# Other start addresses for the SBUF tiles, and two buffers for the local bias tiles

## The chip, the cores and the metric

The kernel runs on one core of one Trainium2 chip. The metric is device time in microseconds (us) for one execution. TensorE (PE; its weight loads are PEld), VectorE (DVE), ScalarE (ACT) and GpSimd (POOL) compute; SyncE (SP) does no arithmetic here and issues most of the DMAs, in program order. SBUF has 128 partitions; every address below is a byte offset within a partition.

## What is computed

Two transformer blocks one after the other on 512 tokens of width 1024, in float32, batch 1:

```
x = first_block(x):   h = rms_norm(x); z = h @ w_in
                      o_fox: 8 heads, causal softmax attention with a forget gate
                      o_nsa: 8 heads; compressed, selected and window attention, summed with gates
                      x += (sigmoid-gated sum of o_fox @ w_br_fox and o_nsa @ w_br_nsa) @ w_out
                      x += relu(rms_norm(x) @ w_ff1)**2 @ w_ff2 ; rms_norm
y = second_block(x):  16 meta tokens ahead of x (528 positions)
                      o_a: 8 heads, sliding window of 128 with sinks and a relative bias
                      o_b: 8 heads on latent keys, each query on its top 256 positions by an index score
                      h += (gate_a * (o_a @ w_branch_a) + gate_b * (o_b @ w_branch_b)) @ w_out
                      h += (silu(rms_norm(h) @ w_gate) * (rms_norm(h) @ w_up)) @ w_down ; rms_norm
```

## The kernel before

Activations lie transposed: eight tiles of 128 features by 512 tokens. To reach float32 accuracy each dense product is three matmuls (`mm3`, line 655): every operand is split into a high part (ScalarE's cast, names in `h`) and a low part (the difference, names in `l`).

All weights stand in HBM as one list of panels (`wall`, 128 partitions x 1024 floats) in the order of use. For each panel there are three steps: `w_load_to` (line 567) issues the DMA into one of three `wr` tiles on SyncE; `w_split_to` (line 604) has ScalarE cast it to `wh` and VectorE or GpSimd subtract to get `wl`, three of each; `dense` (line 660) multiplies, `wh` and `wl` being the stationary operand and an activation tile the moving one of up to 512 columns. Panels are loaded three ahead and split two ahead. A planner in the kernel (`chain`, `pick`, `tick`) keeps a list of small steps with estimated due times and writes them out between the matmuls; it decides the order in which the instructions of every engine stand in the program. It knows nothing of addresses.

SBUF is laid out by pools, in the order in which `build` opens them (lines 2540 to 2546): constants from 16512 to 22784 (`pvt`, `cst` with 640 floats, `ones`, `G` and rings of small tiles), then `rkeep` with two slots of 2112 bytes for the norm factors (`Ra`, `Rb`, `R1`, `Rt`, `Rc`, `Rd`; `Rt` has 528 floats), then the weight pool from 27008 (three each of `wr`, `wh`, `wl`, 4096 bytes), the `tmp` ring from 63872 (four of 2048), and the `u` pool from 72064: 34 slots of 2112 bytes, since the tiles with the meta tokens have 528 floats. The pools of the stages follow from 143872, one set per stage: attention of block 1, FFN 1, attention of block 2, FFN 2. Their `v` slots have 2048 bytes. So, modulo 512: `wr`, `wh`, `wl` and `tmp` start at 384; `rkeep` slots at 256 and 320; `v` slots at 0; `u` slots, 2112 = 4 x 512 + 64 apart, at all multiples of 64.

In block 1's attention and in both gate stages the activations that are multiplied (`xh`, `xl`) are `u` tiles, as `mgh`, `mgl`, `oh`, `ol` are; in both FFNs all of them (`xh`, `xl`, `hh`, `hl`) are `v` tiles. The last eight panels of the second FFN (`2fd*_2`) are split into `u` tiles, named `wk`, and multiplied on halves of 256 columns.

Sliding-window attention of block 2 (`unA_S`, line 2092) runs head by head. Each head needs a bias tile `wa` of 128 x 256, read from DRAM scratch by a DMA on SyncE (`wa_load`, line 2300). Heads 0 and 1 are loaded ahead; head h + 2's load is written at the start of head h:

```python
                if h + 2 < 8:
                    self.wa_load(h + 2)
            nm, l, Pt = u["m"], u["l"], u["P"]
            ...
            wa = self.wa[h]
```

The four VectorE instructions of a head that read it (`P<-pss,wa,nsink`, in `softmax_piece`) come later in the program. `wa` tiles form a ring of three; a load into a slot waits until the slot's last reader is done. Weight loads `wr` stand between the `wa` loads in SyncE's order.

Of the kernel before, what the change touches and what calls it, by code (L numbers as in the profile page):

```python
# [8 lines left out]
F32 = mybir.dt.float32  # L9
# [8 lines left out]
P = 128  # L18
T = 512
# [2 lines left out]
DH = 64  # L22
NMETA = 16
TK = T + NMETA
HT = TK // 2
NEG = -1e30
EPS = 1e-6
# [226 lines left out]
class Prog:  # L254
# [34 lines left out]
    def kk(self, dt=F32):  # L289
        return self.kpool.tile([P, TK], dt, name=self.nm("kk"), tag="kk", bufs=self.nk)  # L290

# [386 lines left out]
    def dense_meta(self, name, evac, M=P, tag="d"):  # L678
# [3 lines left out]
        for k in range(KD):  # L682
# [3 lines left out]
            for n, (w, x) in enumerate(((a, xh), (a, xl), (b, xh))):  # L686
                for e in range(2):
                    self.mms(ps[e][0:M, 0:HT], w, x[:, HT * e:HT * e + HT], k == 0 and n == 0, k == KD - 1 and n == 2)
            yield
        evac(ps)  # L690

    def scaled_meta(self, dst, ps, rows=P, M=NMETA):

        nc = self.nc
        R, w = self.Rf, HT - M
        nc.vector.tensor_mul(dst[0:rows, 0:w], ps[0][0:rows, M:HT], R[0:rows, M:HT])
        nc.vector.tensor_mul(dst[0:rows, w:w + HT], ps[1][0:rows, 0:HT], R[0:rows, HT:TK])
        if M:
# [978 lines left out]
    def x_steps(self, X, m, src, g, sts, pool, meta=False):  # L1677

        if meta:
            hi, lo = self.XM[m] = pool(F32R, (P, TK), name="xh"), pool(F32R, (P, TK), name="xl")  # L1680

# [3 lines left out]
            self.chain(("xm", m), c, after=("mt",), prio=3)  # L1685
            hi, lo = hi[:, NMETA:TK], lo[:, NMETA:TK]
        else:
# [47 lines left out]
    def block1(self):  # L1735
        nc, tc = self.nc, self.tc
        self.XD, self.X, self.merged = {}, self.Xk, {}
        self.xl = tuple(("X", k) for k in range(8))
        self.block1_attention()
        with ExitStack() as c:  # L1740
            self.vpool = c.enter_context(tc.tile_pool(name="vf1", bufs=1))
            self.pk = self.pk2
            self.nv = self.nvf
            x = []
            for k in range(8):
                t = self.u(name="xr")
                nc.scalar.dma_start(t, self.I["xT"][P * k:P * k + P])
                x.append(t)
            self.XD = {}
            self.R = self.rkeep.tile([P, T], F32, name="Rb", tag="R", bufs=2)  # L1750
            self.R2 = self.v(name="R2")
            self.norm("R", 0, self.xl, lambda: self.R[:])
            self.w_out("wo", x, lambda m: self.x_steps(self.XD, m, x[m], self.pv("g_mlp", m), [(0, None)], self.v))
            X2, self.XM = {}, {}
            gg = self.small([P, 8])
            nc.vector.tensor_mul(gg, self.pv("g_final", 0, 8), self.pv("g2", 0, 8))
            x2 = tuple(("x", k) for k in range(8))
            N = {}
            st = {}

            def norms():

                N["R1"] = self.rkeep.tile([P, T], F32, name="R1", tag="R", bufs=2)
                self.Rf = self.rkeep.tile([P, TK], F32, name="Rt", tag="R", bufs=2)
                N["R"] = self.Rf[:, NMETA:TK]
                self.meta_prep(self.Rf)
                self.norm("R1", 0, x2, lambda: N["R1"][:])
                self.norm("pb", 1, x2, None, evac=lambda ps: nc.scalar.copy(N["R"], ps))
                self.chain("Rt", s2, *self.rstd_steps(lambda: st["t"][:], T, D, out=lambda: N["R"][:]), s3,
                           after=("pb", "R1"))  # L1770

            def s2():
                t = st["t"] = self.tmp()
                nc.vector.tensor_mul(t, N["R1"], N["R1"])
                nc.vector.tensor_mul(t, t, N["R"])

            def s3():
                nc.vector.tensor_mul(N["R"], N["R"], N["R1"])

            def after(m):  # L1780
                def store():
                    nc.sync.dma_start(self.xscr[m], x[m])
                return self.x_steps(X2, m, x[m], gg[:, m:m + 1], [(0, None), (1, self.pv("g_final", m))],
                                    self.u, True) + [store]
            self.ffn1(x, after, norms)
            self.ensure(*x2)
            self.R = N["R"]
            self.chain("R", lambda: None, after=("Rt",))
            self.chain("resid", lambda: nc.sync.dma_start(self.rscr, N["R1"]), after=("R1",))
            self.X = lambda k: (self.ensure(("x", k), ("xm", k)), X2[k])[1]  # L1790
# [507 lines left out]
        u["done"](ps)  # L2298

    def wa_load(self, h):  # L2300
        t = self.mpool.tile([P, 256], F32, name=self.nm("wa"), tag="wa", bufs=3)
        self.nc.sync.dma_start(t, self.diagonals(self.v2scr, h, W_UB, 256))
        self.wa[h] = t

# [233 lines left out]
    def build(self):  # L2538
        nc, tc, ctx = self.nc, self.tc, self.ctx
        self.cpool = ctx.enter_context(tc.tile_pool(name="const", bufs=1))  # L2540
        self.rkeep = ctx.enter_context(tc.tile_pool(name="rkeep", bufs=1))
        self.wpool = ctx.enter_context(tc.tile_pool(name="w", bufs=1))
        self.tpool = ctx.enter_context(tc.tile_pool(name="t", bufs=1))
        self.upool = ctx.enter_context(tc.tile_pool(name="u", bufs=1))
        self.dpool = ctx.enter_context(tc.tile_pool(name="dram", bufs=1, space=DRAM))
        self.pp = ctx.enter_context(tc.tile_pool(name="ps", bufs=1, space=PSUM))
        ctx.enter_context(tc.manual_schedule())
        self.pvt = self.cpool.tile([P, NPV], F32, name="pvt")
        nc.sync.dma_start(self.pvt, self.I["vecs"])
        cst = self.cpool.tile([P, T + P], F32, name="cst")  # L2550
        self.cst, self.mw, self.ident = cst, cst[:, 0:T], cst[:, T:T + P]
        self.ones = self.cpool.tile([P, P], F32, name="ones")
        nc.vector.memset(self.ones, 1.0)
        self.one = self.ones[:, 0:1]
        self.tc.nc.scalar.preload_act_table_set("natural_log_exp_and_others")
        self.G = self.cpool.tile([P, 4, 24], F32, name="G")
        self.cscr = self.dpool.tile([8, 6, T], F32R, name="cscr")
        self.xscr = self.dpool.tile([8, P, T], F32, name="xscr")
        self.rscr = self.dpool.tile([P, T], F32, name="rscr")
        self.vascr = self.dpool.tile([8, W_ASC], F32, name="vascr")  # L2560
        self.v1scr = self.dpool.tile([8, 640], F32, name="v1scr")
        self.v2scr = self.dpool.tile([16, W_UB + W_UA], F32, name="v2scr")
        t = self.tmp(F32R)
        nc.vector.memset(t[0:16].bitcast(F32), 1.0)
        nc.gpsimd.dma_start(self.cscr[:, 2], t[0:8])
        nc.gpsimd.dma_start(self.cscr[:, 3], t[8:16])
        self.w_init()
        self.block1()
        self.block2()
# [38 lines left out]
```

## Time and profile before

| | |
|---|---|
| median of 3 runs | 1590.37 us (1586.13 to 1592.13) |
| the profiled execution | 1588.41 us |
| its span, first to last instruction | 1586.6 us |
| busy TensorE, VectorE, ScalarE, GpSimd | 97%, 57%, 49%, 16% |
| mean granted TensorE clock | 0.991 |
| DMA | 149.34 MB, mean 94 GB/s |

A line of the profile names an engine, an operation and its tiles as out<-in, with buffer numbers left out. Line 242 stands at all of them, since a helper records every operation, so the tiles tell them apart. For a matmul the names after the arrow are the moving operand and the stationary one (the weights), in this order.

### The profile page before, as it was taken

The numbers are of one execution on the slowest core, as the hardware profiler recorded it, in microseconds if no ns is written. First come the engines' busy times: TensorE is split into PE (matmuls) and PEld (weight loads), VectorE is DVE, ScalarE is ACT, GpSimd is POOL, SyncE is SP. The second block draws the span as 40 slices with busy tenths as digits, with TensorE's granted clock in tenths as the row PEclk, the third lists the DMA queues.
The fourth block names the chain that finished last, engine by engine and source line by source line (L and its number), as shares of the span: only waits on it lengthen the run. The fifth ranks groups of instructions, "written<-read, shape, count | busy, mean of one in ns | idle before, by whom it ended". The sixth has DMA issues, their size and how long they took to land.

```text
span 1586.6 us, 19934 instructions
## 1 busy us (share of the span) xinstructions
PE 1540.4 (97%) x7400; PEld 1254.5 (79%) x7400; DVE 909.5 (57%) x1781; ACT 775.1 (49%) x1475; POOL 253.3 (16%) x184
## 2 busy tenths in 40 slices
PE   7999999999999999999998899999899999999997
PEld 3788888878878888888877788778687888888887
DVE  5686677762654243455467998576566332336445
ACT  5676687975343232322444784677434222232233
POOL 3343211111210000000044124411131000000001
PEclk9999999999999999999999999999999999999999
DMA  4444321113423333222243222320142223323311
GB/s 154 131 143 137 109 67 61 59 48 101 151 81 99 99 94 93 94 93 93 95 140 79 69 79 82 116 85 14 40 153 94 93 93 99 99 91 109 124 50 54
DMA packets 50545, 149.34 MB, mean 94 GB/s; under 512 B 6652, under 2 KB 10364, under 8 KB 50448
## 3 DMA queue, kind: packets, MB, share of 16 engines
q1 hardware_dynamic: 44496, 138.89, 27.4%
q0 software_dynamic: 3360, 4.46, 1.4%
q10 hardware_dynamic: 2592, 4.72, 0.9%
q8 instruction: 58, 0.95, 0.2%
q14 instruction: 39, 0.32, 0.1%
HBM read 138.37 MB, written 4.67 MB: 90 GB/s over the span
## 4 chain that ended last, share of the span: by engine, by line
PE 88%; DVE 7%; ACT 2%; DMA 2%; issue 1%; SPq 0%; ACTq 0%; POOL 0%; DVEq 0%; POOLq 0%
PE psd L242 74%; PE pss L242 5%; PE pso L242 4%; PE pst L242 4%; DVE sct L242 1%; DVE tmp L242 1%; DVE x L242 1%; DVE sq L242 1%; DMA x<-xT 1%; DVE sm L242 1%; ACT tmp L242 1%; DVE P L242 1%; DVE xl L242 1%; DVE pt L242 0%; ACT xh L242 0%
## 5 line engine op out<-in xcount | busy, mean ns | idle before, releaser
L242 PE MATMUL psd<-xh,wh 128*128 128x512 f32 (+2 forms) x1128 | 452.0, 401 | 8.3 <-ACT xh L242 8.3
L242 PE MATMUL psd<-xh,wl 128*128 128x512 f32 (+2 forms) x1128 | 443.6, 393 | 1.6 <-DVE wl L242 1.6
L242 PE MATMUL psd<-xl,wh 128*128 128x512 f32 (+2 forms) x1128 | 443.9, 394 | 0.4 <-DVE xl L242 0.3
L242 ACT CAST wh<-wr 128x1024 fp32r<-128x1024 f32 (+1 forms) x232 | 241.7, 1043 | 343.6 <-PE psd L242 211.1
L242 POOL TENSOR_TENSOR wl<-wr,wh 128x1024 fp32r<-128x1024 f32 x72 | 178.4, 2478 | 514.3 <-ACT wh L242 467.3
L242 PEld LDWEIGHTS psd<-xh,wh 128*128 128x128 f32 (+1 forms) x1128 | 212.5, 188 | 56.9 <-ACT xh L242 9.8
L242 DVE TENSOR_TENSOR wl<-wr,wh 128x1024 fp32r<-128x1024 f32 (+1 forms) x160 | 196.0, 1225 | 101.2 <-ACT wh L242 99.1
L242 PEld LDWEIGHTS psd<-xh,wl 128*128 128x128 f32 (+1 forms) x1128 | 212.4, 188 | 51.1 <-DVE wl L242 2.0
L242 PEld LDWEIGHTS psd<-xl,wh 128*128 128x128 f32 (+1 forms) x1128 | 212.6, 188 | 47.7 <-issue 2.4
L242 ACT ACTIVATE P<-P,sm 128x256 f32<-128x256 f32 (+7 forms) x319 | 165.8, 545 | 27.0 <-DVE sm L242 26.5
L242 PE MATMUL psd<-hh,wh 128*128 128x512 f32 x384 | 151.6, 395 | 0.0
L242 PE MATMUL psd<-hl,wh 128*128 128x512 f32 x384 | 151.5, 395 | 0.0
L242 PE MATMUL psd<-hh,wl 128*128 128x512 f32 x384 | 151.5, 395 | 0.0
L242 POOL TENSOR_TENSOR sq<-sq,tmp 128x512 f32<-128x512 f32 (+1 forms) x32 | 39.8, 1243 | 429.5 <-ACT tmp L242 426.8
L242 PEld LDWEIGHTS psd<-hh,wh 128*128 128x128 f32 x384 | 72.4, 188 | 17.0
L242 PEld LDWEIGHTS psd<-hh,wl 128*128 128x128 f32 x384 | 72.3, 188 | 16.9
L242 PEld LDWEIGHTS psd<-hl,wh 128*128 128x128 f32 x384 | 72.3, 188 | 16.8
L242 DVE TENSOR_TENSOR pt<-pst,pt 128x384 fp32r<-128x384 f32 (+3 forms) x144 | 69.3, 498 | 16.5 <-ACT pt L242 15.5
L242 ACT ACTIVATE tmp<-psd 128x512 f32<-128x512 f32 x32 | 19.1, 598 | 111.1 <-PE psd L242 111.0
L242 DVE TENSOR_TENSOR tmp<-tmp 128x512 f32<-128x512 f32 (+1 forms) x33 | 22.7, 686 | 87.7 <-ACT tmp L242 87.7
L242 ACT CAST pt<-pst 128x384 fp32r<-128x384 f32 (+3 forms) x144 | 58.5, 439 | 15.8 <-PE pst L242 14.5
L242 PE MATMUL pst<-cst,P 128*128 128x128 f32 (+1 forms) x416 | 62.3, 277 | 2.6 <-DVE pt L242 2.6
(368 smaller groups left out, 2286.2 us busy)
## 6 DMA issues: line engine op xcount, KB each, us to landing
wr<-wall SPq DMA_DIRECT2D x231, 512.0 KB, 3.5
wr<-wall SPq DMA_DIRECT2D x8, 384.0 KB, 3.0
kk<-v2scr SPq DMA_DIRECT2D x8, 264.0 KB, 4.4
x<-xT SPq DMA_DIRECT2D x8, 256.0 KB, 8.4
wb<-v1scr SPq DMA_DIRECT2D x8, 256.0 KB, 3.6
xr<-xT ACTq DMA_DIRECT2D x8, 256.0 KB, 4.5
xscr<-xr SPq DMA_DIRECT2D x8, 256.0 KB, 2.1
x<-xscr ACTq DMA_DIRECT2D x8, 256.0 KB, 4.0
```

The source lines that it names most:

```text
L242: return f(*a, **k)
```

## The change

The row of constants gets 64 floats (256 bytes) of which nothing is used, the norm-factor pool is opened after the `u` pool, `Rt` grows from 528 to 560 floats, and `wa` gets two buffers.

```diff
+CPAD = 64
...
-                self.Rf = self.rkeep.tile([P, TK], F32, name="Rt", tag="R", bufs=2)
+                self.Rf = self.rkeep.tile([P, TK + 32], F32, name="Rt", tag="R", bufs=2)
...
-        t = self.mpool.tile([P, 256], F32, name=self.nm("wa"), tag="wa", bufs=3)
+        t = self.mpool.tile([P, 256], F32, name=self.nm("wa"), tag="wa", bufs=2)
...
         self.cpool = ctx.enter_context(tc.tile_pool(name="const", bufs=1))
-        self.rkeep = ctx.enter_context(tc.tile_pool(name="rkeep", bufs=1))
         self.wpool = ctx.enter_context(tc.tile_pool(name="w", bufs=1))
         self.tpool = ctx.enter_context(tc.tile_pool(name="t", bufs=1))
         self.upool = ctx.enter_context(tc.tile_pool(name="u", bufs=1))
+        self.rkeep = ctx.enter_context(tc.tile_pool(name="rkeep", bufs=1))
...
-        cst = self.cpool.tile([P, T + P], F32, name="cst")
+        cst = self.cpool.tile([P, T + P + CPAD], F32, name="cst")[:, 0:T + P]
```

By these sizes the constants end at 22784 + 256 = 23040 = 45 x 512, and the weight pool starts there; `tmp` starts at 59904 = 117 x 512, the `u` pool at 68096 = 133 x 512, its slots still 2112 apart. The norm factors take 2 x 2240 bytes from 139904 (128 past a multiple of 512; the second slot 320 past one), and the pools of the stages start at 144384 = 282 x 512, 512 bytes above their old start 143872 = 281 x 512. The ring of `wa` gives back 1024 bytes at the end of block 2's pools.

## Rows read from the trace of the kernel before

**Rows 1.** The page: busy time by engine, and shares of the chain that ended last.
```profile
PE 1540.4 (97%) x7400; PEld 1254.5 (79%) x7400; DVE 909.5 (57%) x1781; ACT 775.1 (49%) x1475; POOL 253.3 (16%) x184
...
PE 88%; DVE 7%; ACT 2%; DMA 2%; issue 1%; SPq 0%; ACTq 0%; POOL 0%; DVEq 0%; POOLq 0%
```

**Rows 2.** The chain in order of time: start us, us, what, count.
```profile
347.93 111.72 PE psd L242 x483
...
464.15 314.41 PE psd L242 x1353
...
949.55 14.06 PE psd L242 x61
...
1541.97 16.09 PE psd L242 x134
```

**Rows 3.** Groups by line, TensorE, each form: count, busy us, mean ns, idle before.
```profile
L242 PE MATMUL psd<-xh,wh 128*128 128x512 f32 x1096 | 440.8, 402 | 0.0
...
L242 PE MATMUL psd<-hh,wh 128*128 128x512 f32 x384 | 151.6, 395 | 0.0
...
L242 PE MATMUL psd<-mgh,wh 128*128 128x512 f32 x128 | 50.6, 395 | 0.0
```

**Rows 4.** Groups by line, TensorE's weight loads, each form.
```profile
L242 PEld LDWEIGHTS psd<-hh,wh 128*128 128x128 f32 x384 | 72.4, 188 | 17.0
...
L242 PEld LDWEIGHTS psd<-hh,wk 128*128 128x128 f32 x192 | 29.6, 188 | 0.1
```

**Rows 5.** Groups by line, ScalarE and VectorE, each form.
```profile
L242 ACT CAST hh<-tmp 128x512 fp32r<-128x512 f32 x32 | 19.8, 620 | 1.3 <-DVE tmp L242 1.3
...
L242 ACT CAST hh<-gt 128x512 fp32r<-128x512 f32 x22 | 13.7, 622 | 28.6 <-DVE gt L242 28.6
...
L242 DVE TENSOR_TENSOR wl<-wr,wh 128x1024 fp32r<-128x1024 f32 x158 | 194.8, 1233 | 97.2 <-ACT wh L242 95.2
L242 DVE TENSOR_TENSOR pt<-pst,pt 128x512 fp32r<-128x512 f32 x40 | 27.4, 684 | 0.4 <-ACT pt L242 0.3
...
L242 DVE TENSOR_TENSOR pt<-pst,pt 128x384 fp32r<-128x384 f32 x40 | 22.0, 550 | 8.7 <-ACT pt L242 8.3
L242 DVE TENSOR_TENSOR hl<-tmp,hh 128x512 fp32r<-128x512 f32 x32 | 21.9, 685 | 0.0
...
L242 DVE TENSOR_TENSOR hl<-gt,hh 128x512 fp32r<-128x512 f32 x22 | 15.1, 686 | 1.4 <-ACT hh L242 1.4
```

**Rows 6.** Waits over the span: us in total, times, longest us.
```profile
POOL wl L242 <- ACT wh L242: 467.3, 63, 23.2
...
ACT wh L242 <- DMA wr<-wall: 22.4, 6, 6.0
```

**Rows 7.** Timeline of SyncE's queue in block 2's window attention: start us, us.
```profile
888.80 0.32 SPq L242 DMA_DIRECT2D wa<-v2scr  x1
...
894.06 0.33 SPq L242 DMA_DIRECT2D wa<-v2scr  x1
898.64 0.33 SPq L242 DMA_DIRECT2D wr<-wall  x1
...
909.64 0.33 SPq L242 DMA_DIRECT2D wa<-v2scr  x1
```

**Rows 8.** Timeline of VectorE: the fourth read of heads 3, 4 and 5.
```profile
893.54 0.48 DVE L242 CUSTOM_DVE_ANT_0 P<-pss,wa,nsink 128x256 f32<-128x256 f32 x1
...
909.12 0.48 DVE L242 CUSTOM_DVE_ANT_0 P<-pss,wa,nsink 128x256 f32<-128x256 f32 x1
...
916.85 0.47 DVE L242 CUSTOM_DVE_ANT_0 P<-pss,wa,nsink 128x256 f32<-128x256 f32 x1
```

**Rows 9.** The instructions on `wr`, 870 to 952 us: issue to landing of loads.
```profile
DMA to landing us min/median/max: 3.4/3.8/4.5
```

**Rows 10.** Timeline of ScalarE: casts of the `wr` loads issued at 898.64 and 910.06.
```profile
918.88 1.03 ACT L242 CAST wh<-wr 128x1024 fp32r<-128x1024 f32 x1
...
929.20 1.04 ACT L242 CAST wh<-wr 128x1024 fp32r<-128x1024 f32 x1
```

## Prediction

> **What bounds the kernel now.** I read the busy shares first, then the chain of work that ended last, then that chain in order of time, then the groups of TensorE, and only after these the other engines. TensorE is busy 97% of the span and holds 88% of the chain [rows 1]; every other engine has slack almost everywhere. In order of time the chain shows long pieces with nothing in them but dense matmuls: 111.72 us of 483, 314.41 us of 1353 [rows 2]. A time divided by its count is the distance from one matmul's start to the next, and this rate decides the kernel: 5208 matmuls have 512 columns and take their weights from `wh` or `wl` (3 x 1096, 3 x 384 and 6 x 128; [rows 3] has one row of each count, the 128s being `oh`/`ol` and `mgh`/`mgl`). So an edit of addresses can act in three ways: on TensorE's rate, on an engine that at some moment ends a chain, or through a wait.
>
> **Moved addresses, TensorE.** The diff changes where tiles lie, and one ring's depth. No instruction is added or removed. `wr`, `wh`, `wl` and `tmp` go from 384 bytes past a multiple of 512 to a multiple. The `v` slots of the stages lie at a multiple already (143872 = 281 x 512) and go to another (282 x 512), so for them the change does nothing. The `u` slots, 2112 bytes apart, walk through all eight remainders 0, 64, ..., 448 before and after.
>
> Does the matmul see the remainder? For the moving operand the two long pieces answer. From 347.93 us on (gates, branches, out projection) every moving tile is a `u` tile, spread over all eight remainders: 111.72 / 483 = 0.2313 us each. From 464.15 us on (first FFN) every moving tile is a `v` tile at remainder 0: 314.41 / 1353 = 0.2324 us each [rows 2]. The stage with aligned operands is no faster; it is 0.0011 us slower, which I take as the noise between stages. For the stationary operand, whose address is the one that changes, the row is the last stage: there the weights are the `wk` tiles, which lie in `u` slots at all remainders, and a weight load from them takes 188 ns, as one from `wh` at remainder 384 does [rows 4]. Its matmuls have 256 columns and stand 16.09 / 134 = 0.1201 us apart [rows 2], just over half of 0.2324, so they show no cost of spread weights either. What no row shows is a long stage with both operands aligned. I bound it from both sides. The best rate of any long piece of 512 columns is 14.06 / 61 = 0.2305 us [rows 2]; if alignment brought all 5208 from 0.2324 to it, that is 5208 x 0.0019 = 9.9 us less. In the other direction the spread between the two long pieces gives 5208 x 0.0011 = 5.7 us more. I take 0, because the two pieces that differ in nothing but operands' homes already differ by that little, in the direction against alignment.
>
> **Moved addresses, ScalarE, VectorE, GpSimd.** ScalarE casts `hh` from `tmp` (remainder 384) in 620 ns and from `gt` (a `v` tile, remainder 0) in 622 ns; VectorE's subtraction takes 685 and 686 ns for the same pair [rows 5]. Reading at 384 costs nothing. For the wide `wl` subtraction there is no aligned twin, so I extrapolate from aligned tiles: 512 columns 684 ns, 384 columns 550 ns, so 1.05 ns a column and 684 + 512 x 1.05 = 1220 ns for 1024, against 1233 ns measured [rows 5]. At most 13 ns x 158 = 2.1 us of VectorE's time could come back. It would not reach the chain: GpSimd waits 467.3 us in all for the cast in front of its share of these subtractions [rows 6], so the weight preparation runs ahead of its use. GpSimd's own `wl` has no aligned row; by the same pair of engines I take 0, and a loss there would fall into the same 467 us. The norm factors `R` move from remainders 256 and 320 to 128 and 320; they are read by the same VectorE operations that show no dependence. Sum of this part: 0.
>
> **Moved addresses, DMA.** A weight load lands 3.4 to 4.5 us after its issue [rows 9]. ScalarE waits for weight loads 6 times, 22.4 us in all [rows 6], and DMA holds 2% of the chain [rows 1]. The `x` tiles go to `u` slots, which only exchange remainders. I take 0; the bounds of this term lie inside those of TensorE's. [...]
>
> **Two buffers for `wa`.** This is the only edit that changes a wait. `wa_load(h + 2)` is called as head h starts, before head h's own bias is read. With three buffers the load takes the slot of head h - 1. The trace shows that a load waits for the last reader of its slot: the one at 894.06 us (head 6) goes out as the fourth `P<-pss,wa` of head 3 ends at 893.54 + 0.48 [rows 7, 8]. With two buffers it takes the slot of head h itself, so SyncE must hold it until the fourth read of head h, which stands later in the program. SyncE issues in order, so queued behind it are the weight loads `wr`, and for these ScalarE's cast `wh`, GpSimd's `wl`, then TensorE.
>
> The load at 888.80 (head 5) would wait until 894.02, the same end of head 3's reads, and hold the `wr` behind it 5.2 us [rows 7, 8]. The load at 894.06 is the worst: it waits for the fourth read of head 4, 909.12 + 0.48 = 909.60, and the `wr` behind it, issued at 898.64 before, goes at 909.60 + 0.33 = 909.9, so 11.3 us late [rows 7, 8]. With at most 4.5 us to land [rows 9] it is there at 914.4. Its cast starts at 918.88 [rows 10]: 4.5 us of cover are left. The load at 909.64 (head 7) waits for 916.85 + 0.47 = 917.32 [rows 7, 8], 7.7 us, and the `wr` behind it has landed at 917.3 + 0.4 + 4.5 = 922.2, against a cast at 929.20 [rows 10]. The earlier heads' loads find less behind them. The bias itself comes in time: it leaves at the end of head h's reads and is wanted a whole head later, and from head 4's fourth read to head 5's are 7.7 us [rows 8], more than the 4.5 us in which even a four times larger `wr` lands. So the hold is hidden: cost 0; if the cover were gone, up to 11.3 us, the whole lateness of that load. Nothing is gained by the shallower ring, so the lower end is 0 too.
>
> **Sum.** 0 on each term. The profiled execution took 1588.41 us (span 1586.6 and 1.8 around it); the median of the runs shown is 1590.37, 2.0 above it, and those runs span 6 us. I predict 1589.0, between the two.
>
> **Rivals.** *Alignment does speed TensorE up.* For it: weights are the one operand that no long stage shows at a multiple of 512 together with an aligned moving tile. Against it: the moving operand shows no gain, and a weight load takes 188 ns from any remainder. Worth 9.9 us: 1588.4 - 9.9 = 1578.5. Chance 0.13.
>
> *SyncE's hold surfaces (slower).* The place is head 6's `wa`, with the weight load behind it; it decides from the point where the hold exceeds 918.88 - 4.5 - 898.64 = 15.7 us, against 11.3 now. Then ScalarE stands at a cast in order, and the exponentials of the softmax behind it stop the heads. For it: 11.3 of that load's 15.7 us of cover go at one stroke. Against it: the 4.5 us left. Priced at the full lateness: 1588.4 + 11.3 = 1599.7. Chance 0.09.
>
> *The change doesn't do what it says*: `v` slots are aligned before, `u` slots never become so. That is so by the addresses, and it ends with the forecast's time.
>
> **How the numbers follow.** The forecast, no change, has 0.78. 0.5% is 8 us, about what a measurement of this kernel can tell from none, so the rival of 9.9 us counts as faster and that of 11.3 us as slower. Range: from the faster rival's 1579 to the slower one's 1600, which leaves out the parts of both that go further.
>
> **What would show it.** Right: the FFN pieces of the chain stay at 0.231 to 0.233 us a matmul; weight loads of TensorE stay at 188 ns; `wl` on VectorE between 1220 and 1235 ns; the last three bias loads go out right after the fourth read of the head two before, at about 894, 910 and 917 us; one weight load near 910 rather than 899, and its cast near 919 all the same. Wrong: a rate of 0.230 or less in the FFN (the faster rival), or ScalarE waiting for a weight load between 900 and 930 us (the slower one).

## The result, and the profile after

The changed kernel takes 1573.86 us (median of 5 runs, 1569.97 to 1577.27) against 1591.11 us before (5 runs): a ratio of 0.9895, 95% interval 0.9868 to 0.9922. The forecast was 1589.0, in a range from 1579 to 1600; the time lies below the range and on the side of the faster rival. The profiled execution took 1570.39 us, 18.02 less than the one before.

The page of the profile after: the span, busy time by engine, and the DMA group of the weight loads (KB each, median us to landing).

```profile
span 1568.6 us, 19935 instructions
...
PE 1519.6 (97%) x7400; PEld 1249.2 (80%) x7400; DVE 908.5 (58%) x1781; ACT 775.4 (49%) x1475; POOL 253.6 (16%) x184
...
wr<-wall SPq DMA_DIRECT2D x231, 512.0 KB, 3.5
```

Against [rows 1] TensorE has 20.8 us less of busy time with the same 7400 matmuls, and VectorE, ScalarE and GpSimd have changed by at most 1.0 us. So the matmuls themselves became faster. Which ones, the chain in order of time says (start us, us, what, count):

```profile
346.20 112.71 PE psd L243 x483
...
463.41 306.72 PE psd L243 x1353
...
771.82 38.23 PE psd L243 x168
...
941.19 14.06 PE psd L243 x61
...
1199.94 321.69 PE psd L243 x1419
...
1523.85 16.10 PE psd L243 x134
```

Of the kernel before, two pieces that did not stand among its rows:

```profile
780.25 39.14 PE psd L242 x168
...
1210.00 329.76 PE psd L242 x1419
```

The pieces answer one to one to [rows 2]. The first FFN goes from 314.41 to 306.72 us for the same 1353 matmuls, 0.2324 to 0.2267 us each; the second from 329.76 to 321.69 for 1419, again 0.2324 to 0.2267. Those are 7.69 and 8.07 us. Add 0.91 from the piece of 168, which are the last products of the first FFN (`hh` and `hl`, `v` tiles), 0.74 by which the first FFN starts earlier, and 0.72 spread over the stages between. The sum is 18.13 us; the starts of the last stage (1541.97 and 1523.85) lie 18.12 apart. The 61 matmuls at 941.19 and the last stage, both with `u` tiles as one operand, have their old times.

The groups by form show the same split. First TensorE after (count, busy us, mean ns, idle before), then its weight loads:

```profile
L243 PE MATMUL psd<-xh,wh 128*128 128x512 f32 x1096 | 438.2, 400 | 0.0
...
L243 PE MATMUL psd<-hh,wh 128*128 128x512 f32 x384 | 149.5, 389 | 0.0
...
L243 PE MATMUL psd<-mgh,wh 128*128 128x512 f32 x128 | 50.6, 395 | 0.0
```

```profile
L243 PEld LDWEIGHTS psd<-hh,wh 128*128 128x128 f32 x384 | 72.1, 188 | 14.8
L243 PEld LDWEIGHTS psd<-hh,wk 128*128 128x128 f32 x192 | 29.7, 189 | 0.1
```

`hh` (a `v` tile) falls from 395 to 389 ns a matmul, the 6 ns by which the rate fell; `mgh` (a `u` tile) stays at 395; `xh` is `v` in some stages and `u` in others and falls by 2 [rows 3]. A weight load has the same 188 ns, or 189 from `wk` [rows 4]: whatever was gained doesn't show in the load's own time.

One piece of the chain got longer, that of 483 matmuls of the `u` stage, 111.72 to 112.71. Its windows (columns: PE, PEld, DVE, ACT, POOL, granted clock, DMA share, GB/s) say why, after:

```profile
346.20:350.00 3.80, 3.80 (x14) 3.02 (x14) 2.51 (x3) 2.05 (x3) 0.00 (x0) 0.73 0.00 0
362.20:442.20 80.00, 80.00 (x348) 64.93 (x347) 38.97 (x48) 36.34 (x49) 18.22 (x8) 1.00 0.38 124
```

and before:

```profile
347.93:352.00 4.07, 4.07 (x19) 3.29 (x19) 2.51 (x3) 2.05 (x3) 0.00 (x0) 1.00 0.09 15
...
363.93:443.93 80.00, 80.00 (x348) 64.93 (x347) 39.77 (x49) 37.35 (x51) 18.21 (x8) 1.00 0.36 119
```

In its first 3.80 us the clock granted was 0.73, and 14 matmuls ran; before, 19 ran in 4.07 us at 1.00. Just ahead of it, from 342 us on, TensorE was busy for 3.19 of 4.20 us at a granted clock of 0.84, and in the 7 us before that for 5.72 at 1.00. The 80 us from 16 us behind the start hold 348 matmuls in both. That 1 us is the clock, not the addresses: in the next four experiments, two of them with the weights at multiples of 512, this piece takes 111.72 to 111.74 us.

### The profile page after: what moved, and what is told of

It is laid out like the page before. It is cut to its first block, busy times and chain, and to the rows that moved or that the text cites. A ratio compares the mean times of both kernels' runs of the same rounds, so it can differ in the third digit from the quotient of the medians.

```text
span 1568.6 us, 19935 instructions
## 1 busy us (share of the span) xinstructions
PE 1519.6 (97%) x7400; PEld 1249.2 (80%) x7400; DVE 908.5 (58%) x1781; ACT 775.4 (49%) x1475; POOL 253.6 (16%) x184
## 4 chain that ended last, share of the span: by engine, by line
PE 87%; DVE 8%; ACT 2%; DMA 2%; issue 1%; SPq 0%; ACTq 0%; POOL 0%; DVEq 0%; POOLq 0%
PE psd L243 74%; PE pss L243 5%; PE pst L243 4%; PE pso L243 4%; DVE sct L243 1%; DVE tmp L243 1%; DVE sq L243 1%; DVE x L243 1%; DVE xl L243 1%; DVE sm L243 1%; DVE pt L243 0%; DMA x<-xT 0%; DVE P L243 0%; DMA R<-rscr 0%; ACT xh L243 0%
```

## The experiments

The theories at the start. *Alignment* (the faster rival taken at its word): a matmul is faster when both operands lie at multiples of 512 bytes. *One operand*: only the weights, or only the moving tile, decide. *Difference*: neither address counts, but the stationary start minus the moving start, modulo some power of two. Before, weights at 384 and `v` tiles at 0 differ by 128 modulo 256; after, by 0. In the list below a rate is a chain piece of the first FFN (1353 matmuls) divided by its count.

**Only the `wa` ring.**

```diff
-        t = self.mpool.tile([P, 256], F32, name=self.nm("wa"), tag="wa", bufs=3)
+        t = self.mpool.tile([P, 256], F32, name=self.nm("wa"), tag="wa", bufs=2)
```

> The kernel before with the ring of wa tiles cut to two and every address of weights and stage tiles as before. Theory A (the gain is TensorE's rate, which is faster only where the weight tile and the moving tile both start at a multiple of 512): time as before, ratio 0.998 to 1.002, FFN pieces of the chain at 0.2324 us a matmul; the bias loads wait for the fourth read of the head two before, near 894, 910 and 917 us, and TensorE does not notice. Rival W (the changed order of waits on SyncE's queue gives the gain): ratio 0.989 and FFN pieces still at 0.2324, the time coming back between 850 and 950 us.

Measured: 1588.85 against 1589.14 us, ratio 0.9998 (0.9989 to 1.0008). SyncE's timeline is the one that the prediction drew (start us, us):

```profile
887.37 6.52 SPq L242 DMA_DIRECT2D wa<-v2scr  x2
893.98 0.86 SPq L242 DMA_DIRECT2D wr<-wall  x2
909.36 0.33 SPq L242 DMA_DIRECT2D wa<-v2scr  x1
909.78 0.38 SPq L242 DMA_DIRECT2D wr<-wall  x1
```

and ScalarE's casts:

```profile
918.60 1.03 ACT L242 CAST wh<-wr 128x1024 fp32r<-128x1024 f32 x1
...
928.94 1.04 ACT L242 CAST wh<-wr 128x1024 fp32r<-128x1024 f32 x1
```

The weight load that went at 898.64 [rows 7] now goes at 909.78, 11.1 us later, and its cast stays at 918.60 against 918.88 [rows 10]. So the hold exists and is hidden, and the shallower ring gives nothing back.

**Only the alignment**, with three `wa` buffers. The padding of the constants is taken out and a ring of small tiles shortened instead, so that there is room; `rkeep` is opened behind the `u` pool, as in the change. Weights start at 22528 and `v` tiles at 143872, both multiples of 512.

```diff
-        return self.cpool.tile(list(shape), dt, name=self.nm("sm"), tag="sm%d" % n, bufs=bufs)
+        return self.cpool.tile(list(shape), dt, name=self.nm("sm"), tag="sm%d" % n, bufs=6 if n == 32 else bufs)
...
-                self.Rf = self.rkeep.tile([P, TK], F32, name="Rt", tag="R", bufs=2)
+                self.Rf = self.rkeep.tile([P, TK + 32], F32, name="Rt", tag="R", bufs=2)
```

> The kernel after with three wa buffers again; the constants are shortened by 256 bytes instead of lengthened (a ring of small tiles, of which two are ever used, gets 6 slots instead of 8), so the weights start at 22528 = 44 x 512 and the stage pools at 143872 = 281 x 512. Theory A: the whole gain, ratio 0.989 to 0.991, FFN pieces at 0.2267 us a matmul. Rival W: ratio 1.000.

Measured: 1573.26 us, ratio 0.9899 (0.9885 to 0.9914), the whole effect.

```profile
464.63 306.72 PE psd L243 x1353
```

**Weights at a multiple of 512, `v` tiles 256 past one.** The changed kernel with `Rt` at its old size.

```diff
-                self.Rf = self.rkeep.tile([P, TK + 32], F32, name="Rt", tag="R", bufs=2)
+                self.Rf = self.rkeep.tile([P, TK], F32, name="Rt", tag="R", bufs=2)
```

> The kernel after without the 32 spare floats in Rt: weights still start at a multiple of 512, the v slots of the stages 256 bytes past one. Theory A: the gain is gone, FFN pieces at 0.231 to 0.233 us a matmul, ratio 0.998 to 1.002. Rival S (the weight tiles alone matter: a stationary operand at a multiple of 512): FFN pieces at 0.2267, ratio 0.989 to 0.991. Rival H (a multiple of 256 is enough for the moving operand): the same numbers as S.

Measured: 1573.98 us, 0.9904 (0.9883 to 0.9926), the rate of the changed kernel:

```profile
461.05 306.72 PE psd L243 x1353
```

So `v` tiles need not be at a multiple of 512: *alignment* falls as far as the moving operand goes.

**Nothing aligned.** The kernel before with two `wa` buffers and 96 unused floats behind the `u` pool: weights stay at 384 past a multiple of 512, `v` tiles go to 384 too.

```diff
         self.upool = ctx.enter_context(tc.tile_pool(name="u", bufs=1))
+        self.gap = ctx.enter_context(tc.tile_pool(name="gap", bufs=1)).tile([P, 96], F32, name="gap")
```

> The kernel before with two wa buffers and 384 unused bytes behind the u pool, so that weights and v slots both start 384 bytes past a multiple of 512. Theory A: FFN pieces at 0.230 to 0.233, ratio 0.998 to 1.002. Rival D (only the difference of the two addresses modulo 512 matters): FFN pieces at 0.2267, ratio 0.989 to 0.991.

Measured: 1572.9 us, 0.9894 (0.9875 to 0.9913).

```profile
463.09 306.73 PE psd L242 x1353
```

This run decides. No weight or `v` tile is aligned, the weights lie where they lay before, and the gain is complete. Only the difference to the moving tile is another. *Alignment* and *weights alone* fall; *moving tile alone* had fallen already, since `v` tiles at a multiple of 512 were slow before and are fast in the changed kernel. *Difference* stands.

**The rates by pair, alone.** A kernel of nothing but matmuls, 70 groups of 72: eight stationary tiles `sA` to `sH` at 0, 64, ..., 448 modulo 512 against eight moving ones `mA` to `mH`, and tiles `I` and `J` 16 and 32 bytes past 0.

```diff
+            for i in range(N):
+                o, q = sf + P * (i // 3 % 8), mf + T * (i % 3)
+                nc.tensor.matmul(ps, s[:, o:o + P], m[:, q:q + T], start=i == 0, stop=i == N - 1,
+                                 skip_group_check=True)
```

> A kernel that leaves out all of the computation: 70 groups of 72 matmuls of 512 columns and nothing beside them. Moving tiles mA to mH start 0, 64, ..., 448 bytes past a multiple of 512, stationary tiles sA to sH likewise; all 64 pairs run. In six further groups mI, sI start 16 and mJ, sJ 32 bytes past one. Theory A (both at a multiple of 512) is already against the runs with weights at 0 and v slots at 256, and with both at 384; it would show one fast pair of 64, mA with sA. Theory M (the difference of the two starts must be a multiple of 256): 16 fast pairs at 0.2267 us, the 8 with equal starts and the 8 that differ by 256, and 48 at 0.230 to 0.233. Rival D (the difference must be a multiple of 512): 8 fast pairs. Rival L (what costs is a change of the moving tiles' remainder from one matmul to the next, or other engines' traffic, not the pair): all 64 pairs alike.

Groups by form (moving, stationary; count, busy us, mean ns of one):

```profile
L49 PE MATMUL ps<-mA,sB 128*128 128x512 f32 x72 | 17.0, 395 | 0.0
...
L49 PE MATMUL ps<-mD,sA 128*128 128x512 f32 x72 | 17.0, 394 | 0.0
...
L49 PE MATMUL ps<-mA,sC 128*128 128x512 f32 x72 | 16.9, 394 | 0.0
...
L49 PE MATMUL ps<-mB,sA 128*128 128x512 f32 x72 | 16.7, 392 | 0.0
L49 PE MATMUL ps<-mA,sD 128*128 128x512 f32 x72 | 16.6, 391 | 0.0
...
L49 PE MATMUL ps<-mA,sE 128*128 128x512 f32 x72 | 16.5, 389 | 0.0
...
L49 PE MATMUL ps<-mC,sC 128*128 128x512 f32 x72 | 16.5, 389 | 0.0
```

The distance from start to start, averaged over a group without its first four matmuls, has four values over 63 of the 64 pairs, to 0.1 ns (to 0.4 in the first group of each moving tile). The 64th pair, `mA,sA`, is the first group of the run: its first matmuls stand 427 ns apart, its later ones 226.7.

```
stationary minus moving, modulo 256     0       64      128     192
ns from matmul to matmul, 512 columns   226.7   233.4   232.2   228.9
```

0 is what the FFNs have after (0.2267) and 128 what they had before (0.2324). Pairs 256 apart (`mA,sE`) are as fast as equal ones, so at steps of 64 the period is 256. That makes the 16 fast pairs of theory M; rivals D (8) and L (all alike) fall. The other 48 pairs reach from 228.9 to 233.4, a little further down than the 230 that was expected. The finer tiles agree at 32 bytes (both 32 past: 226.7; one alone: 233.3) and not at 16: with both 16 past, and so no difference, 230.0.

**The other two differences in the kernel.** As the run with nothing aligned, with 48 and with 16 floats in the gap: differences of 192 and 64.

```diff
+        self.gap = ctx.enter_context(tc.tile_pool(name="gap", bufs=1)).tile([P, 48], F32, name="gap")
```

> The kernel before with two wa buffers and 192 unused bytes behind the u pool: weights 384 and v slots 192 bytes past a multiple of 512, a difference of 192. Theory M (the rate depends on the stationary start minus the moving start modulo 256, with the four rates of the grid: 0 gives 0.2267 us, 64 gives 0.2334, 128 gives 0.2323, 192 gives 0.2289): FFN pieces at 0.2289 to 0.2291, so 2772 x 0.0034 = 9.4 us less than before, ratio 0.994. Rival Z (fast or not fast, nothing between, in a kernel whose other engines are busy too): 0.2267 and 0.989, or 0.232 and 1.000.

```diff
+        self.gap = ctx.enter_context(tc.tile_pool(name="gap", bufs=1)).tile([P, 16], F32, name="gap")
```

> The same with 64 unused bytes: weights at 384, v slots at 64, a difference of 320, which is 64 modulo 256. Theory M: the worst of the four, FFN pieces at 0.2334, 2772 x 0.0010 = 2.8 us more than before, ratio 1.001 to 1.003. Rival Z: 0.2324 as before, ratio 1.000.

Measured with 48: 1577.59 us, 0.9943 (0.9924 to 0.9962), 0.2289 us a matmul.

```profile
465.18 309.70 PE psd L242 x1353
```

With 16: 1591.72 us, 1.002 (1.0007 to 1.0034), 0.2333 us a matmul.

```profile
463.52 315.69 PE psd L242 x1353
```

Both rates are the grid's, so rival Z falls, and the second makes the kernel slower than before, as the grid says.

**Finer steps, alternating pairs, fewer columns.** Matmuls alone again: steps of 16 bytes (`A` to `P` at 0, 16, ..., 240), two pairs in turn (`px`, `py`), and 256 (`pu`) and 128 columns (`pw`).

```diff
+        group("px", [(0, 0), (4, 4)], n=144)
+        group("py", [(0, 4), (4, 0)], n=144)
+        for d in range(4):
+            group("pu", [(0, 4 * d)], w=256)
+        for d in range(4):
+            last = group("pw", [(0, 4 * d)], w=128)
```

> A kernel that leaves out all of the computation, matmuls alone, as the grid before. Stationary tiles sA to sP start 0, 16, ..., 240 bytes past a multiple of 512 against moving mA at 0, then moving mA to mP likewise against sA; then two alternations (px: mA with sA, mE with sE, both 64 past; py: mA with sE, mE with sA), and 256 and 128 columns at differences 0, 64, 128, 192. Theory N (the moving operand meets the load of the next weights): px is slow, near the mean of the rates at 64 and 192, (0.2334 + 0.2289) / 2 = 0.231, and py fast at 0.2267. Theory O (the moving operand meets its own weights): px 0.2267 and py 0.231. By 16 bytes: steps within each 64 bytes for the moving operand (16 past gave 0.2317 in the grid), none or small ones for the stationary one. The loss per column shrinks in proportion: 256 columns lose half of what 512 lose.

```profile
L37 PE MATMUL px<-mA,sA 128*128 128x512 f32 x72 | 28.5, 395 | 0.0
L37 PE MATMUL py<-mE,sA 128*128 128x512 f32 x72 | 28.3, 394 | 0.0
L37 PE MATMUL py<-mA,sE 128*128 128x512 f32 x72 | 28.3, 393 | 0.0
L37 PE MATMUL px<-mE,sE 128*128 128x512 f32 x72 | 28.3, 392 | 0.0
...
L37 PE MATMUL ps<-mA,sI 128*128 128x512 f32 x72 | 17.0, 395 | 0.0
...
L37 PE MATMUL ps<-mI,sA 128*128 128x512 f32 x72 | 16.9, 395 | 0.0
...
L37 PE MATMUL pu<-mA,sI 128*128 128x256 f32 x72 | 8.8, 283 | 0.1
L37 PE MATMUL pu<-mA,sA 128*128 128x256 f32 x72 | 8.8, 283 | 0.0
L37 PE MATMUL pu<-mA,sM 128*128 128x256 f32 x72 | 8.7, 281 | 0.1
L37 PE MATMUL pu<-mA,sE 128*128 128x256 f32 x72 | 8.5, 278 | 0.1
```

From start to start: with the moving tile at 0, only stationary tiles at 0, 16 and 240 reach 226.7 ns; 192 gives 228.9, 208 to 224 and 32 to 176 lie between 229.9 and 234.3. One of these values contradicts the grid: `mA,sI`, a difference of 128, has 233.4 here, where all 16 such pairs of the grid have 232.2 to 232.4; `mI,sA`, a difference of -128, has 232.3. So at 128 the rate isn't settled by the difference alone, and no run shows what settles it. For the moving operand the values are 231.6 at 16, 228.9 at 64 and 226.7 at 240, and for the stationary one the steps are not small, so the expectation by 16 bytes was wrong in its second half.

With `px` both pairs in turn have a difference of 0, and yet it is 233.3 ns from `mA,sA` to `mE,sE` and 229.9 back, 231.6 on average; with `py`, whose pairs differ by 64 and 192, it is 231.2 and 232.1, 231.7 on average. Theory N asked for a slow `px` and a fast `py`, theory O for the reverse; both are slow, so neither holds. The matmul's own pair isn't enough: what comes before or after it counts too, and 226.7 was seen only where all matmuls in a row keep one difference.

With 256 columns the order turns: 0 is slowest with 119.9, 64 fastest with 113.4, 128 and 192 have 118.6 and 117.8. The expectation that 256 columns lose half was wrong. With 128 columns all four take 111.6 to 111.7.

**The `u` stages too.** Slots of 2048 bytes, so that `u` tiles keep one difference to the weights. For that the 16 meta columns leave the tiles, and a product on 528 columns is no longer two of 264 but one of 512 and one of 16. The rest is as in the change, but with 544 floats in `Rt` and three `wa` buffers.

```diff
-            for n, (w, x) in enumerate(((a, xh), (a, xl), (b, xh))):
-                for e in range(2):
-                    self.mms(ps[e][0:M, 0:HT], w, x[:, HT * e:HT * e + HT], k == 0 and n == 0, k == KD - 1 and n == 2)
+            pairs = zip((a, a, b), *((x[0], x[1], x[0]) for x in (self.XM[k], self.X(k))))
+            for n, (w, m, x) in enumerate(pairs):
+                for p, y, c in ((ps[0], m, NMETA), (ps[1], x, T)):
+                    self.mms(p[0:M, 0:c], w, y, k == 0 and n == 0, k == KD - 1 and n == 2)
...
-            hi, lo = self.XM[m] = pool(F32R, (P, TK), name="xh"), pool(F32R, (P, TK), name="xl")
+            hi, lo = pool(F32R, name="xh"), pool(F32R, name="xl")
+            mh, ml = self.XM[m] = self.xmh[:, m], self.xml[:, m]
```

> The kernel after with the u slots at a pitch of 2048 instead of 2112 bytes, so that every u tile too starts at a multiple of 512, as the weights do (v slots 256 past one, a difference that the grid shows as fast). For this the 16 meta columns of X2 lie in two small tiles of their own, and each of the four products with the meta tokens takes matmuls of 512 and 16 columns instead of two of 264; three wa buffers. Theory M: the pieces with u tiles as moving operand go from 0.2313 us a matmul (0.2334 in the profile of the change) to 0.2267; some 2230 matmuls x 0.0046 = 10 us on top of the change, ratio to before 0.982 to 0.985. Rival L (u tiles are slow because moving tiles alternate): the pieces stay at 0.231 and the ratio at 0.989.

Measured: 1580.53 us (1576.62 to 1598.88), 0.9974 (0.9939 to 1.0008): no faster than before by more than the measurement tells, and slower than the changed kernel. The ratio of 0.982 to 0.985 that was expected did not come: the rate came, the time didn't. The chain in order of time:

```profile
349.22 109.58 PE psd L243 x483
...
836.21 0.34 PE pss L243
836.55 0.01 PE psd L243
836.56 0.34 PE pss L243
...
1210.79 321.69 PE psd L243 x1419
```

The changed kernel in the same products:

```profile
840.87 0.12 PE pss L243
840.99 0.12 PE psd L243
841.11 0.12 PE pss L243
```

The `u` stage of block 1 runs at 109.58 / 483 = 0.2269 us, against 0.2313 [rows 2]: there the theory holds as well, and rival L falls. But the second FFN starts 10.85 us later than in the changed kernel (1210.79 and 1199.94). A pair of products takes 0.35 us (836.21 to 836.56) where two of 264 columns took 0.24 (840.87 to 841.11), and there are 96 such pairs: 96 x 0.11 = some 10 us, lost to small matmuls that I had priced by their columns. The rest is not settled: the planner writes another order, and one long piece, behind 24.70 us of which TensorE was busy for 20.23, begins with a granted clock of 0.52 in its first 2.82 us (columns as above):

```profile
998.18:1001.00 2.82, 2.82 (x8) 2.17 (x8) 1.40 (x3) 1.59 (x4) 0.00 (x0) 0.52 0.00 0
```

## Why the prediction was wrong

**Moved addresses, TensorE: the step that failed.** It asked "Does the matmul see the remainder?" of the moving operand and of the stationary one, each by itself, and answered no for each. In truth a matmul sees each remainder, but only against the other one: in the grid every start of either operand appears with all four rates, and which of them comes hangs on the difference of the two starts, which the step never formed. So the term that was put at 0 was 16.7 us. The change turned the difference from 128 to 0 modulo 256 for every matmul of a `v` tile with `wh` or `wl`, which is both FFNs but for the last eight panels, and their chain pieces of 1353, 1419 and 168 matmuls lost 7.69 + 8.07 + 0.91 us of the 18.1.

**The comparison that misled.** 0.2313 with spread `u` tiles against 0.2324 with aligned `v` tiles was read as "The stage with aligned operands is no faster". But only the moving operand was aligned in it, and the `u` stage runs through all four differences. Their grid values have a mean of 230.3 ns, and two pairs in turn (`px`, `py`) came out at 231.6 and 231.7, so its 231.3 is no yardstick for either operand. With one difference throughout, the same stage reaches 226.9 (the experiment with `u` slots of 2048 bytes). The `v` stage had one difference throughout, and the second slowest. What was taken "as the noise between stages" was the effect itself, averaged on one side.

**The bound.** 0.2305 us, the best long piece, was taken as the best that alignment could reach. That piece is a `u` stage too (its 14.06 / 61 is unchanged after), so a mean over differences. 9.9 us thus was no bound. The faster rival was right in its sign, but too small, with 17.3 us between the medians, and wrong in its cause: with nothing aligned the gain was the same. That its place and its sign fitted is partly luck, since two aligned operands happen to have a difference of 0. The rate named as its sign, 0.230 or less in the FFN, came, at 0.2267.

**The row of the last stage.** `wk` tiles at all remainders with a weight load of 188 ns [rows 4] and 0.1201 us a matmul [rows 2] were the evidence that the stationary address doesn't count. Two flaws: the load's 188 ns is blind to the effect, as it is 188 or 189 before and after alike; and 256 columns order the differences the other way, so nothing follows from them for 512.

**Moved addresses, other engines: right.** The casts and subtractions after, against [rows 5]:

```profile
L243 DVE TENSOR_TENSOR wl<-wr,wh 128x1024 fp32r<-128x1024 f32 x158 | 194.8, 1233 | 93.5 <-ACT wh L243 91.3
...
L243 DVE TENSOR_TENSOR hl<-tmp,hh 128x512 fp32r<-128x512 f32 x32 | 21.9, 683 | 0.0
```

The 13 ns that an aligned `wl` might have given did not come: 1233 as before. `hh<-tmp` keeps its 620 ns.

**Moved addresses, DMA: right as far as a trace tells.** Weight loads land 3.5 us after their issue in the median of the page's group, before as after.

**Two buffers for `wa`: right.** The load at 910 rather than 899, the cast at 919 all the same, and 0 for the time are shown by the run with that edit alone. One bound was too small. The "at most 4.5 us to land" are of the kernel before; in the changed kernel, where two weight loads go out right behind a held bias load, the instructions on `wr` from 866 to 948 us show up to 6.0:

```profile
DMA to landing us min/median/max: 3.4/4.5/6.0
```

The cover was enough for that too: ScalarE waits for no weight load between 860 and 930 us.

**The rival of SyncE's hold** did not come: the hold is there and ends 4.3 us before it would be felt (909.78 + 4.5 of [rows 9] against 918.60; with 6.0 it would be 2.8). *The change doesn't do what it says* was told wrongly as well: "`v` slots are aligned before" is true and said nothing, since with the weights moved the pair changed.

## What to carry to other kernels

Where TensorE is the bound, take the rate of each dense stage from the chain (time over count) and look at the difference of both operands' start addresses before either one; a stage whose tiles lie at mixed addresses is no yardstick, since it is a mean. When a pool's pitch or order is to be chosen anyway, give weights and moving tiles of the float32r stages with 512 columns the same remainder modulo 256: here that was worth 1%, with no instruction changed, and a gap of 384 unused bytes did it. A layout that needs other instructions to get there has to be priced by those first, as the `u` slots of 2048 bytes showed.

## What the runs showed of the hardware

- A 512-column matmul in float32r stands 226.7, 233.4, 232.2 or 228.9 ns from the next for differences of 0, 64, 128 and 192 bytes modulo 256 between the starts of its stationary and moving tiles; the fast value was seen only in a row of matmuls with one difference, and at 128 one group of a second run had 233.4. 16 bytes to either side of the stationary start keep 226.7 for a moving tile at 0; a moving tile 16 past a stationary one at 0 has 231.7, so in steps of 16 bytes the difference alone no longer tells the rate.
- With 256 columns the same differences give 119.9, 113.4, 118.6 and 117.8 ns, so of these four the fast difference for 512 columns is the slowest for 256 (one group of 72 each).
- With 128 columns a matmul stands 111.6 to 111.7 ns from the next at all four differences, and one of 16 columns is hardly cheaper: some 0.35 - 0.23 = 0.12 us for its half of a pair.
- Why the difference counts, and why modulo 256, stays open.
